# An encoder layer on one core: longer runs of wide matmuls in the feed-forward, merged products for its fourth tile, and another order of the last normalisation

## The chip, the cores and the metric

The kernel runs on one core of a Trainium2 chip. The metric is the device time of one execution in microseconds (us). A core has four compute engines with an instruction stream each: TensorE (PE in the profile, its weight loads PEld), VectorE (DVE), ScalarE (ACT) and GpSimd (POOL); SyncE (SP) issues most of the DMAs. SBUF is the on-chip memory, PSUM the eight banks of 512 f32 a partition into which TensorE accumulates.

## The reference, cut to what matters

One layer on 512 tokens of width 2048: a normalisation, an input projection, two token mixers side by side, an output projection, and then the gated feed-forward block with a width of 5632, which is where the change lies, and a last normalisation.

```python
    xn = rms_norm(x, ffn_norm_g[l])
    up = jnp.einsum("bsd,df->bsf", xn, w_up[l])
    up = depthwise_conv(up, ffn_dw_w[l], ffn_dw_b[l])
    gate, val = jnp.split(up, 2, axis=-1)
    x = x + jnp.einsum("bsf,fd->bsd", jax.nn.silu(gate) * val, w_down[l])
return rms_norm(x, final_norm_g)
```

## The kernel before, in words

All matrices are f32. Each operand is split in two parts, a high one in the rounded type that TensorE multiplies at full rate and a low one that holds the rest; a product is high x high + low x high + high x low. Weights come in units of 128 x 1024 values (512 KB): SyncE loads a unit `raw`, ScalarE copies its high part (`whi`, L117), VectorE subtracts to get the low part (`wlo`, L121). There are four buffers each for `whi` and `wlo`, and `weights()` makes units three ahead of the one in use. For some units VectorE first adds two raw ones (`ws`, L712 to L723).

**The up-projection.** The feed-forward runs over f = 0..43; each f is 128 gate and 128 value columns, and tokens are taken in two halves of 256. A scheme of the Strassen kind makes an f's four block products from seven products (0 to 6), each over eight k-steps. Its right-hand operands `xc` lie ready in SBUF, each k-step as 512 columns: the high part of 256 tokens beside their low part. There are two forms:

- `up` (merged): for each k-step one wide matmul of 512 columns (L773, the high weights times both parts at once) and one narrow matmul of 256 columns (L779, the low weights times the high part), which adds into the second half of the same bank. The halves are added later: ScalarE copies second halves out (`pl`, and `vv`; L805), and VectorE does eleven adds (L820 to L844). Within `up` the products go in runs: (0,1), (2,3), (4,5), (6). All but the last product of a run give their eight wide matmuls first; the last one gives one wide matmul, then come the narrow ones of the run, then the last product's other seven wide ones, so that a bank never closes with a narrow matmul of another.
- `up_apart`: three matmuls of 256 columns for each k-step (L131, L135, L136) into half a bank; three copies on ScalarE, six adds on VectorE (L879 to L885). It is used for f = 0 and f = 3.

A product's bank is one of three `mm` banks, the `po` bank or one of two `tr` banks (`product_bank`); from f = 4 on product 6 takes `po`, the others the `mm` banks.

**The down-projection.** Four f's are a chunk. While a chunk is worked, the four hidden tiles of the one before (each split in `hh` and `hl`, L911 and L912) are multiplied with `w_down`: behind product 3 and behind product 6 of each f one unit, which is two output tiles of 24 matmuls in all (`down`; L131 high x high, L135 high x low part `hl`, L136 low weights `wlo`), in the two `tr` banks. ScalarE copies each bank out (`pdc`, L926), and a GpSimd-queue DMA adds it to the sum in HBM (L927). The last chunk leaves out some of these places: f = 40 has none, f = 43 none behind product 3.

**The tail.** The last normalisation's factor is worked out by `spread` and 384 tokens are finished feature-major, in ten tiles on VectorE (L999) and six on GpSimd (L997); SyncE sends them to `out_T` in pairs (L1001, L1003). The other 128 tokens go to `out_N`. A planner orders each engine's instructions by priority and its own estimate of when operands are ready, so that rows move when code is written in another order; `pin` holds an instruction where the code has it.

## Time and profile before

| | |
|---|---|
| time, median of 3 runs (lowest, highest) | 2016.16 us (2015.9, 2017.13) |
| the profiled execution | 2016.15 us, its span 2014.4 us, 1.75 us outside the span |
| TensorE busy | 2004.4 us (100%) |
| VectorE busy | 1667.9 us (83%) |
| ScalarE busy | 1054.7 us (52%) |
| granted TensorE clock | 0.998 of full speed |
| wide matmuls of the up-projection | 2352, from 682.3 to 1937.0 us |

In the rows, a time is the start in us from the span's begin, followed by the duration in us; `x16` is a count; `pu<-xc,whi` reads "the tile pu is written from xc and whi"; a bracket at a row's end says how long the engine was idle before it and what released it. In the chain of waits each piece's length is the time to the next piece.

### The profile page before, as it was taken

To read this page: it belongs to the slowest core of one execution; us is meant where nothing else is said; L and a number is where in the kernel's file an instruction comes from. 1 tells how busy PE (TensorE), PEld (TensorE's weight loads), DVE (VectorE), ACT (ScalarE), POOL (GpSimd) and SP (SyncE) were. 2 spreads that over 40 slices of the span, in tenths; PEclk is the share of its full clock that TensorE was granted. 3 is DMA by queue.
4 is the path that set the end of the run, shared out by engine and by line. 5 is a ranking of instruction groups with operands and counts; after the bars stand their busy time and mean duration, and the time that the engine had idled before them with its cause. 6 is when DMAs were issued, how large, how long until landed. Compare 5 with 4: busy or idle time off the path is not lost.

```text
span 2014.4 us, 28027 instructions
## 1 busy us (share of the span) xinstructions
PE 2004.4 (100%) x10510; PEld 1715.7 (85%) x10510; DVE 1667.9 (83%) x2264; ACT 1054.7 (52%) x1689; POOL 169.4 (8%) x201
## 2 busy tenths in 40 slices
PE   9999999999999999999999999999999999999998
PEld 8888888888888998888888888888888888888887
DVE  7996888987576898887888888888888888889875
ACT  6323344476355665555555554555555555555563
POOL 0000000000002101111111111111111111110111
PEclk9999999999999999999999999999999999999999
DMA  7233333346348766556556556555565566564573
GB/s 258 84 106 93 113 95 107 105 139 211 100 136 213 189 163 152 139 129 152 133 135 148 131 131 154 132 139 141 127 145 145 127 145 147 131 141 128 145 206 129
DMA packets 98567, 284.25 MB, mean 141 GB/s; under 512 B 11008, under 2 KB 11520, under 8 KB 98432
## 3 DMA queue, kind: packets, MB, share of 16 engines
q1 hardware_dynamic: 71712, 231.07, 37.4%
q0 software_dynamic: 26720, 51.40, 17.1%
q8 instruction: 83, 1.36, 0.3%
q14 instruction: 52, 0.43, 0.1%
HBM read 227.90 MB, written 54.53 MB: 140 GB/s over the span
## 4 chain that ended last, share of the span: by engine, by line
PE 99%; DMA 0%; ACT 0%; DVE 0%; ACTq 0%; issue 0%; DVEq 0%
PE pu L773 27%; PE pu L779 14%; PE pd L136 8%; PE pd L131 8%; PE pd L135 8%; PE pj L131 6%; PE pj L135 6%; PE pj L136 6%; PE po L131 3%; PE po L135 3%; PE po L136 3%; PE pv L342 1%; PE pv L341 1%; PE pv L340 1%; PE po L535 1%; PE trp L518 1%
## 5 line engine op out<-in xcount | busy, mean ns | idle before, releaser
L117 ACT ACTIVATE whi<-raw 128x1024 fp32r<-128x1024 f32 x364 | 384.5, 1058 | 480.4 <-PE pj L135 131.7
L121 DVE TENSOR_TENSOR wlo<-raw,whi 128x1024 fp32r<-128x1024 f32 x364 | 444.5, 1222 | 208.5 <-ACT whi L117 198.0
L773 PE MATMUL pu<-xc,whi 128*128 128x512 f32 x2352 | 580.0, 391 | 0.0
L773 PEld LDWEIGHTS pu<-xc,whi 128*128 128x128 f32 x2352 | 433.5, 188 | 83.0
L779 PEld LDWEIGHTS pu<-xc,wlo 128*128 128x128 f32 x2352 | 306.8, 191 | 14.6
L779 PE MATMUL pu<-xc,wlo 128*128 128x256 f32 x2352 | 311.3, 283 | 0.0
L136 PE MATMUL pd<-hh,wlo 128*128 128x512 f32 x640 | 250.3, 391 | 0.0
L131 PE MATMUL pd<-hh,whi 128*128 128x512 f32 x640 | 249.7, 390 | 0.0
L135 PE MATMUL pd<-hl,whi 128*128 128x512 f32 x640 | 249.1, 390 | 0.0
L927 POOL DMA_DIRECT2D x2d<-pdc x160 | 138.9, 870 | 1099.0 <-ACT pdc L926 870.1
L131 PE MATMUL pj<-xh,whi 128*128 128x512 f32 x512 | 198.3, 392 | 0.1
L136 PE MATMUL pj<-xh,wlo 128*128 128x512 f32 x512 | 198.2, 390 | 0.0
L135 PE MATMUL pj<-xl,whi 128*128 128x512 f32 x512 | 198.2, 390 | 0.0
L805 ACT ACTIVATE pl<-pu 128x256 f32<-128x256 f32 x294 | 109.9, 382 | 150.1 <-PE pu L773 142.8
L117 ACT ACTIVATE whi<-ws 128x1024 fp32r<-128x1024 f32 x132 | 139.7, 1058 | 72.6 <-PE pu L773 54.2
L396 DVE SCALAR_TENSOR_TENSOR y<-ch,prm,y 128x501 f32<-128x501 f32 (+14 forms) x240 | 173.5, 740 | 4.4
L121 DVE TENSOR_TENSOR wlo<-ws,whi 128x1024 fp32r<-128x1024 f32 x132 | 161.2, 1221 | 14.8 <-ACT whi L117 14.8
L136 PEld LDWEIGHTS pd<-hh,wlo 128*128 128x128 f32 x640 | 120.1, 188 | 28.5 <-DVE wlo L121 3.3
L135 PEld LDWEIGHTS pd<-hl,whi 128*128 128x128 f32 x640 | 120.2, 188 | 25.0 <-DVE hl L912 0.4
L131 PEld LDWEIGHTS pd<-hh,whi 128*128 128x128 f32 x640 | 120.4, 188 | 22.6
L926 ACT ACTIVATE pdc<-pd 128x512 f32<-128x512 f32 x160 | 93.8, 588 | 79.1 <-PE pd L136 66.0
L131 PEld LDWEIGHTS pj<-xh,whi 128*128 128x128 f32 x512 | 96.0, 188 | 20.7 <-ACT g L276 0.3
(228 smaller groups left out, 2721.1 us busy)
## 6 DMA issues: line engine op xcount, KB each, us to landing
raw<-in_w_up SPq DMA_DIRECT2D x176, 512.0 KB, 3.9
raw<-in_w_down SPq DMA_DIRECT2D x88, 512.0 KB, 4.0
x2d<-pdc POOLq DMA_DIRECT2D x160, 256.0 KB, 4.8
raw<-in_w_in SPq DMA_DIRECT2D x60, 512.0 KB, 3.7
raw<-in_w_out SPq DMA_DIRECT2D x32, 512.0 KB, 3.6
raw<-in_w_v SPq DMA_DIRECT2D x16, 512.0 KB, 4.2
tab<-in_tab SPq DMA_DIRECT2D x32, 256.0 KB, 4.9
x<-in_xT SPq DMA_DIRECT2D x16, 256.0 KB, 6.1
```

Of the source, the lines that this page charges most:

```text
L117: i = nc.scalar.activation(hi[:, :n], raw[:, :n], AF.Copy)
L121: j = nc.vector.tensor_sub(lo[:, :n], raw[:, :n], hi[:, :n].bitcast(F32))
L131: m = nc.tensor.matmul(ps, hi[:, a], mh, start=start, stop=False)
L135: nc.tensor.matmul(ps, hi[:, a], ml, start=False, stop=False)
L136: return nc.tensor.matmul(ps, lo[:, a], mh, start=False, stop=stop)
L340: nc.tensor.matmul(ps, xh, wh[:, f], start=kk == 0, stop=False)
L396: nc.vector.scalar_tensor_tensor(y[:, a:b], h[:, a + j - PAD:b + j - PAD], prm[:, o + j:o + j + 1], y[:, a:b], op0=ALU.mult, op1=ALU.add)
L773: i = nc.tensor.matmul(ps, w[0][:, k * P:(k + 1) * P], comb[c][k], start=k == 0, stop=stop and k == ks[-1])
L779: i = nc.tensor.matmul(ps[:, H:], w[1][:, k * P:(k + 1) * P], comb[c][k][:, :H], start=False, stop=stop and k == U - 1)
L805: nc.scalar.activation(to, ps, AF.Copy)
L926: nc.scalar.activation(t, ps, AF.Copy)
L927: nc.gpsimd.dma_start(xd[d], t, accum_op=ALU.add)
```

## The change

There are four parts.

1. In `up`, from f = 4 on, the runs are (0,1,2,3) and (4,5,6) in place of (0,1), (2,3), (4,5), (6). Products 3 and 6 both take the `po` bank then, the others `mm`.
2. f = 3 uses `up` in place of `up_apart`, with the short runs.
3. `down` (in its usual form) opens both of its banks first, gives all sixteen matmuls with the high weights (L933 of the new file), and then the eight with the low weights (L943).
4. In `spread` for the tail, VectorE writes the factor to SBUF, and ScalarE copies it to PSUM; before, VectorE wrote it to PSUM and ScalarE copied it to SBUF. In `finish`, VectorE's first tile (d = 0) takes the factor from SBUF, its others take it from PSUM; GpSimd takes it from SBUF as before. ScalarE's scaling for d = 2 is held in its place.

```diff
@@ spread
+        nc.vector.scalar_tensor_tensor(r, q, 1.5, r, op0=ALU.add, op1=ALU.mult)
         if both:
-            nc.vector.scalar_tensor_tensor(ps, q, 1.5, r, op0=ALU.add, op1=ALU.mult)
-            nc.scalar.activation(r, ps, AF.Copy)
+            nc.scalar.activation(ps, r, AF.Copy)
             return ps, r
-        nc.vector.scalar_tensor_tensor(r, q, 1.5, r, op0=ALU.add, op1=ALU.mult)
         return r
@@ product_bank
-        at = n % 6 if f < CH else 3 * (c == 6)
+        at = n % 6 if f < CH else 3 * (c % 3 == 0 and c > 0)
@@ up
+        runs = ((0, 1), (2, 3), (4, 5), (6,)) if f < CH else ((0, 1, 2, 3), (4, 5, 6))
...
-            if c == 6:
+            run = next(r for r in runs if c in r)
+            if len(run) == 1:
                 ps = bank(c)
                 wides(c, w, ps, range(U - 1))
                 lows(c, w, ps)
                 i = wides(c, w, ps, range(U - 1, U), stop=True)
-            elif c % 2:
+            elif c == run[-1]:
                 ps = opened.pop(c)
                 lows(c, w, ps)
                 i = wides(c, w, ps, range(1, U), stop=True)
             else:
-                ps, opened[c + 1] = bank(c), bank(c + 1)
-                wides(c, w, ps, range(U))
-                wides(c + 1, made[weights.at], opened[c + 1], range(1))
+                if c == run[0]:
+                    for j in run:
+                        opened[j] = bank(j)
+                        wides(j, w if j == c else made[weights.at + j - c - 1], opened[j],
+                              range(1 if j == run[-1] else U))
+                ps = opened.pop(c)
                 i = lows(c, w, ps, stop=True)
@@ hidden
-        return gated_tile(f, *(up_apart if f == CH - 1 else up)(f, between))
+        return gated_tile(f, *up(f, between))
@@ down
-            for d in range(d0, d0 + U // CH):
-
-                ps = (psm.tile([P, S], F32, tag="mm", name="pd") if wide and d % 5 > 1 else
-                      psa.tile([P, S], F32, tag="tr", name="pd", bufs=2))
+            two = range(d0, d0 + U // CH)
+            banks = [] if wide else [bank(d) for d in two]
+            for ps, d in zip(banks, two):
                 for k in range(CH):
-                    mm3(ps, w, (d - d0) * CH + k, *hs[k], k == 0, k == CH - 1)
+                    a = slice(((d - d0) * CH + k) * P, ((d - d0) * CH + k + 1) * P)
+                    for i, x in enumerate(hs[k]):
+                        nc.tensor.matmul(ps, w[0][:, a], x, start=k + i == 0, stop=False)
+            for d in two:
+                if wide:
+                    ps = bank(d)
+                    for k in range(CH):
+                        mm3(ps, w, (d - d0) * CH + k, *hs[k], k == 0, k == CH - 1)
+                else:
+                    ps = banks[d - d0]
+                    for k in range(CH):
+                        a = slice(((d - d0) * CH + k) * P, ((d - d0) * CH + k + 1) * P)
+                        nc.tensor.matmul(ps, w[1][:, a], hs[k][0], start=False, stop=k == CH - 1)
@@ finish
-    def finish(pair, r, apart=False, split=False):
+    def finish(pair, rb, apart=False, split=False):
...
             if apart:
-                nc.scalar.activation(x, x, AF.Copy, scale=g)
-                nc.gpsimd.tensor_mul(o[:, i], x, r)
+                j = nc.scalar.activation(x, x, AF.Copy, scale=g)
+                if d == 2:
+                    pin(j)
+                nc.gpsimd.tensor_mul(o[:, i], x, rb[1])
             else:
-                nc.vector.scalar_tensor_tensor(o[:, i], x, g, r, op0=ALU.mult, op1=ALU.mult)
+                nc.vector.scalar_tensor_tensor(o[:, i], x, g, rb[d == 0], op0=ALU.mult, op1=ALU.mult)
```

How the order of instructions moves is shown at four places. The first is TensorE in an f from the middle of the feed-forward, before: the end of one down unit, products 0 to 3, and the beginning of the next down unit (`pd<-hh` is a hidden tile's high part, `pd<-hl` its low part).

```order
L136 MATMUL pd<-hh,wlo 128x512
L773 MATMUL pu<-xc,whi 128x512 x9
L779 MATMUL pu<-xc,wlo 128x256 x16
L773 MATMUL pu<-xc,whi 128x512 x16
L779 MATMUL pu<-xc,wlo 128x256 x16
L773 MATMUL pu<-xc,whi 128x512 x7
L131 MATMUL pd<-hh,whi 128x512
L135 MATMUL pd<-hl,whi 128x512
L136 MATMUL pd<-hh,wlo 128x512
```

The same place of an f after the change.

```order
L943 MATMUL pd<-hh,wlo 128x512 x8
L773 MATMUL pu<-xc,whi 128x512 x25
L779 MATMUL pu<-xc,wlo 128x256 x32
L773 MATMUL pu<-xc,whi 128x512 x7
L933 MATMUL pd<-hh,whi 128x512
L933 MATMUL pd<-hl,whi 128x512
```

Two runs of sixteen narrow matmuls became one of 32, and the low weights' matmuls of a down unit, which stood as every third one, stand at its end in one run of eight. Behind products 4 to 6 the same holds: before, it is 16 and 8 narrow ones, after, 24.

The second place is TensorE at the first down unit of the feed-forward, behind product 3 of f = 4, before the change, with buffer numbers: `hl_6633` is the low part of the fourth hidden tile (f = 3), `pd_6739` and `pd_6755` are the two banks.

```order
L131 MATMUL pd_6755<-hh_6628,whi_6665 128x512
L135 MATMUL pd_6755<-hl_6629,whi_6665 128x512
L136 MATMUL pd_6755<-hh_6628,wlo_6666 128x512
L135 MATMUL pd_6739<-hl_6633,whi_6665 128x512
L136 MATMUL pd_6739<-hh_6632,wlo_6666 128x512
L131 MATMUL pd_6755<-hh_6632,whi_6665 128x512
```

After the change, the same place; there `hl_6592` is the fourth tile's low part, `pd_6698` and `pd_6699` are the banks.

```order
L933 MATMUL pd_6699<-hh_6591,whi_6642 128x512
L773 MATMUL pu_6741<-xc_4982,whi_6657 128x512
L933 MATMUL pd_6698<-hl_6592,whi_6642 128x512
L933 MATMUL pd_6699<-hl_6592,whi_6642 128x512
L943 MATMUL pd_6698<-hh_6579,wlo_6643 128x512
L943 MATMUL pd_6698<-hh_6583,wlo_6643 128x512
```

The first matmul that wants the fourth tile's low part was the 20th of the unit's 24 before. Now it is the 15th, and one wide matmul of product 4 is drawn forward in front of it, so that it has fifteen matmuls of the unit's time ahead of it.

The third place is VectorE at the end of f = 3, before the change: the adds of `up_apart` and the weights around them.

```order
L879 TENSOR_TENSOR vl<-vv,pu 128x512
L723 TENSOR_TENSOR ws<-ws,raw 128x1024
L881 TENSOR_TENSOR uu<-uu,pu 128x256
L882 TENSOR_TENSOR vl<-vl,uu 128x512
L121 TENSOR_TENSOR wlo<-ws,whi 128x1024
L121 TENSOR_TENSOR wlo<-raw,whi 128x1024
L883 TENSOR_TENSOR vv<-vv,uu 128x256
L121 TENSOR_TENSOR wlo<-ws,whi 128x1024
```

After the change, the same place.

```order
L824 TENSOR_TENSOR vv<-vv,pl 128x512
L722 TENSOR_TENSOR ws<-ws,raw 128x1024
L831 TENSOR_TENSOR uu<-pu,pl 128x256
L834 TENSOR_TENSOR uu<-pu,pl 128x256
L832 TENSOR_TENSOR vl<-vv,uu 128x512
L121 TENSOR_TENSOR wlo<-ws,whi 128x1024
L121 TENSOR_TENSOR wlo<-raw,whi 128x1024
L837 TENSOR_TENSOR uu<-uu,pu 128x256
L121 TENSOR_TENSOR wlo<-ws,whi 128x1024
```

From the first row of it up to the fourth tile's low part (L912 before, L916 after) VectorE has five adds more than before, and two weight adds (L712 and L719 before) in other places.

The last place is VectorE's own first tiles of the tail, before, with the factor `st` in PSUM.

```order
L202 TENSOR_SCALAR st<-q,rstd_18246 128x384
L999 TENSOR_SCALAR fin<-x_17681,prm,st 128x384
L999 TENSOR_SCALAR fin<-x_17683,prm,st 128x384
L999 TENSOR_SCALAR fin<-x_17689,prm,st 128x384
L999 TENSOR_SCALAR fin<-x_17691,prm,st 128x384
```

And after.

```order
L201 TENSOR_SCALAR rstd_18205<-q,rstd_18205 128x384
L1020 TENSOR_SCALAR fin<-x_17640,prm,rstd_18205 128x384
L1020 TENSOR_SCALAR fin<-x_17642,prm,st 128x384
L1020 TENSOR_SCALAR fin<-x_17648,prm,st 128x384
L1020 TENSOR_SCALAR fin<-x_17650,prm,st 128x384
```

The first tile has the factor `rstd` in SBUF as its operand, the others `st` in PSUM, which ScalarE fills now. On GpSimd the first two tiles changed places (d = 3 ahead of d = 2); SyncE's order is the same.

More of the change, by code (lines that the diff above doesn't have):

```diff
@@ L915, in down, with bank @@
     def down(hs, ds, wide=False):
+        def bank(d):
+            return (psm.tile([P, S], F32, tag="mm", name="pd") if wide and d % 5 > 1 else
+                    psa.tile([P, S], F32, tag="tr", name="pd", bufs=2))
         for d0 in ds:
             w = weights()
-            for d in range(d0, d0 + U // CH):
-                ps = (psm.tile([P, S], F32, tag="mm", name="pd") if wide and d % 5 > 1 else
-                      psa.tile([P, S], F32, tag="tr", name="pd", bufs=2))
+            two = range(d0, d0 + U // CH)
+            banks = [] if wide else [bank(d) for d in two]
+            for ps, d in zip(banks, two):
                 for k in range(CH):
-                    mm3(ps, w, (d - d0) * CH + k, *hs[k], k == 0, k == CH - 1)
+                    a = slice(((d - d0) * CH + k) * P, ((d - d0) * CH + k + 1) * P)
[11 more added lines that the diff above has]
+                        nc.tensor.matmul(ps, w[1][:, a], hs[k][0], start=False, stop=k == CH - 1)
                 t = t2("pdc")
@@ L1032, in along @@
             pairs.remove(at)
-            finish(at, rb[at % 3 == 1], at % 3 == 1, at in (0, 2))
+            finish(at, rb, at % 3 == 1, at in (0, 2))
     for g, ps in enumerate(banks):
```

## The prediction

> **What bounds the kernel now.** The page's head, the busy times and the chain that ended last come first, then the line view of the wide matmuls.
>
> ```profile
> span 2014.4 us, 28027 instructions
> PE 2004.4 (100%) x10510; PEld 1715.7 (85%) x10510; DVE 1667.9 (83%) x2264; ACT 1054.7 (52%) x1689; POOL 169.4 (8%) x201
> PE 99%; DMA 0%; ACT 0%; DVE 0%; ACTq 0%; issue 0%; DVEq 0%
> L773 PE MATMUL pu<-xc,whi x2352: 389/389/404, 682.3 to 1937.0; 128*128 128x512 f32 x196
> ```
>
> TensorE is the chain: 99% of the span. An edit counts by the matmuls it removes, by what a matmul costs beyond its columns, and by the waits of TensorE that it makes or takes. So the chain is read next, piece by piece: a piece's length is the time to the next piece. Here are f = 2 (merged, short runs), f = 3 (apart), and the start of f = 4; and, as a ruler, nine wide matmuls inside a down unit's end.
>
> ```profile
> 701.78 2.29 PE pu L773 x10
> 704.07 1.91 PE pu L779 x16
> 705.98 3.65 PE pu L773 x16
> ...
> 717.12 3.20 PE pu L773 x14
> 720.32 0.95 PE pu L779 x8
> 721.27 0.23 PE pu L773
> 721.62 0.12 PE pu L135
> ...
> 741.06 0.12 PE pu L135
> 741.66 2.07 PE pu L773 x9
> ...
> 819.11 2.04 PE pu L773 x9
> ```
>
> A wide matmul takes 2.04 / 9 = 0.227 us, a narrow one 0.12. f = 3 takes 168 x 0.12 = 20.16 us (721.50 to 741.66). A merged f has 56 of each: 56 x (0.2267 + 0.12) = 19.41. f = 2 lasts from 701.78 to 721.50, 19.72 us; its pieces are 57 wide and 56 narrow, 12.92 + 6.72 = 19.64. The rest, 0.08 us over four runs of narrow matmuls, is 0.02 us a run, whether the run has 8 or 16. Between first and last wide matmul there were 4176 wide matmuls (the down-projection's have the same 512 columns) and 2520 narrow ones in 187 runs: 1249.0 us without any extra, against 1937.0 - 682.3 = 1254.7. So 5.7 us are extras: 187 x 0.02 = 3.7 and about 1.9 in waits. The view of waits and the chain around one of them say where those lie.
>
> ```profile
> PEld pd L136 <- DVE wlo L121: 3.3, 9, 0.4
> 841.71 0.23 PE pd L131
> 841.94 0.43 PE pd L136
> 842.37 0.23 PE pd L131
> ```
>
> Nine times a down unit's third or fourth matmul wants low weights that VectorE has not yet made. Weight loads run ahead of matmuls, so the 3.3 us of that row are not all lost: in the chain the piece is 0.43 instead of 0.23, 0.20 us lost, and nine times that is 1.8. With the rest above (5.7 - 3.7) I take 1.9.
>
> **The change, part by part.** (a) *f = 3 merged.* 20.16 becomes 19.41: -0.75 us, and its four runs are in (b). ScalarE gets six more copies of 256 columns and VectorE five more adds; ScalarE was busy for 10.22 of f = 3's 20 us (row below), so its part costs nothing; VectorE's part is (d).
>
> (b) *Longer runs.* From f = 4 on there are 2 runs instead of 4 in each of 40 f's, or 80 fewer; some others go because the order no longer draws wide matmuls into narrow runs; f = 3 adds its own. Counted in the order, 187 become 94 over the whole stretch, 93 x 0.02 = -1.9 us. The bounds are 0 (the 0.02 might belong to each bank rather than to a switch) and -1.9; f = 2's rest is the same in every run, so I take -1.9.
>
> (c) *Low weights last in a down unit.* They are wanted sixteen matmuls, 3.6 us, later than the high ones instead of 0.5 us later. The lateness was 0.2 us each: all nine waits go, -1.9 us. Late next would be the units of a run: the first product's wide matmuls ask for four high parts within 25 matmuls (5.7 us), where they asked for two within 9, and TensorE could catch up with ScalarE's copies. ScalarE is little loaded and VectorE has 5 us idle in a usual f (24.88 busy of 30):
>
> ```profile
> 721.00:741.00 20.00, 20.00 (x168) 19.96 (x167) 18.86 (x26) 10.22 (x14) 1.74 (x2) 1.00 0.71 178
> 741.00:772.00 31.00, 31.00 (x166) 26.56 (x165) 30.64 (x41) 17.51 (x29) 2.61 (x3) 1.00 0.55 155
> 772.00:802.00 30.00, 30.00 (x160) 25.93 (x159) 24.88 (x32) 16.40 (x25) 3.47 (x4) 1.00 0.62 138
> 1845.00:1860.00 15.00, 15.00 (x91) 13.34 (x90) 14.93 (x21) 8.32 (x12) 0.00 (x0) 1.00 0.43 133
> ```
>
> (The columns: stretch, length, then the busy time of PE, PEld, DVE, ACT and POOL, TensorE's clock, DMA share, GB/s.) Walked through with the durations of the rows below, the parts of a usual f come 6 us and more ahead of their matmuls; no cost.
>
> (d) *The new wait, at f = 4.* From 721 to 772 us VectorE has hardly any idle time (18.86 of 20, 30.64 of 31), and five adds are put in ahead of the fourth hidden tile's low part, which f = 4's first down unit now wants as its fifteenth matmul. VectorE's rows there, before, and TensorE's:
>
> ```profile
> 721.34 0.28 PE L131 MATMUL pu<-xc,whi 128*128 128x256 f32 x1
> 733.09 0.68 DVE L879 TENSOR_TENSOR vl<-vv,pu 128x512 f32<-128x512 f32 x1
> 738.21 1.22 DVE L121 TENSOR_TENSOR wlo<-raw,whi 128x1024 fp32r<-128x1024 f32 x1
> 739.35 0.42 DVE L883 TENSOR_TENSOR vv<-vv,uu 128x256 f32<-128x256 f32 x1
> 739.68 1.22 DVE L121 TENSOR_TENSOR wlo<-ws,whi 128x1024 fp32r<-128x1024 f32 x1
> 742.62 0.68 DVE L903 TENSOR_TENSOR vl<-vl,rstd 128x512 f32<-128x512 f32 x1
> 743.22 0.69 DVE L902 TENSOR_TENSOR g<-g,rstd 128x512 f32<-128x512 f32 x1
> 746.09 0.75 DVE L893 SCALAR_TENSOR_TENSOR uy<-g,prm,uy 128x511 f32<-128x511 f32 x1
> 746.75 0.75 DVE L893 SCALAR_TENSOR_TENSOR uy<-vl,fwn,uy 128x511 f32<-128x511 f32 x1
> 753.42 0.69 DVE L912 TENSOR_TENSOR hl<-uy,hh 128x512 fp32r<-128x512 f32 x1
> 754.21 0.44 PE L135 MATMUL pd<-hl,whi 128*128 128x512 f32 x1
> ```
>
> From start to start, VectorE takes 1.14 us for 1024 columns (738.21 to 739.35), 0.60 for 512 (742.62 to 743.22), 0.33 for 256 (739.35 to 739.68) and 0.66 for a convolution step (746.09 to 746.75). In the order after, from the add that takes the place of 733.09's to the end of the fourth low part, stand ten of 1024, ten of 512, seven of 256, four convolution steps and the low part itself (0.69): 11.4 + 6.0 + 2.3 + 2.6 + 0.7 = 23.0, so it is done at 756.1. TensorE: f = 3 from 721.34, 19.49 with its four runs, f = 4 from 740.83; then 32 wide and 32 narrow matmuls (11.09 + 0.02), so the down unit begins at 751.94, and the matmul in question, fifteen matmuls on, is due at 755.34. A matmul starts 0.1 us after such a writer's end (753.42 + 0.69 to 754.21), and its piece was 0.1 longer than a wide one's: 756.2 + 0.1 - 755.34 = 1.0 us. Bounds: 0 (VectorE had gaps of its own before, up to 1.1 us, which the walk may have too little or too much of) and 2 (one more 1024-column step in front, 1.14). I take +1.0; it is the middle, and the walk gives it. Behind the waiting matmul stand the eight low-weights ones and f = 4's products 4 to 6; all slide by the same 1.0, paid once.
>
> (e) *The tail.* In order: VectorE's factor, GpSimd's and VectorE's tiles, SyncE's first DMAs, and the stretch in which the DMA engines stand still once more.
>
> ```profile
> 1998.31 0.57 DVE L202 SCALAR_TENSOR_TENSOR st<-q,rstd 128x384 f32<-128x384 f32 x1
> 1999.49 3.24 DVE L999 SCALAR_TENSOR_TENSOR fin<-x,prm,st 128x384 f32<-128x384 f32 x6 [0.62 <-ACT rstd L203]
> 1999.55 2.98 POOL L997 TENSOR_TENSOR fin<-x,rstd 128x384 f32<-128x384 f32 x3 [36.60 <-ACT rstd L203]
> 2000.14 0.86 SPq L1001 DMA_DIRECT2D out_T<-fin  x2
> 2001.58 0.33 SPq L1003 DMA_DIRECT2D out_T<-fin  x1
> 2002.00:2003.00 1.00, 1.00 (x8) 0.83 (x8) 1.00 (x3) 0.52 (x2) 1.00 (x2) 1.00 0.68 260
> ```
>
> Both engines waited for ScalarE's copy; the factor itself was there at 1998.88. VectorE's first tile can now start 0.58 us earlier (1999.49 to 1998.91), and so the first DMA. The end is set by the transfers, which run without a break from 2001 on but for 0.32 us in the last row. That break is the third DMA's: it waits in SyncE's order for GpSimd's second tile (1999.55 + 2 x 1.0 = 1.55, issue at 1.58). So the tail gets shorter only as GpSimd gets earlier. If GpSimd starts at 1998.9 too, it is -0.55 us; if it starts at 1999.5 as before, the first DMAs' gain becomes a longer break and it is 0. No row has VectorE and GpSimd both starting on two SBUF operands (VectorE's tiles read the factor from PSUM), so neither end is excluded; I take 0, the nearest row's start.
>
> The Trainium skill (SBUF — State Buffer, "Who interferes with whom") speaks against a gain: a VectorE instruction with two SBUF inputs and a GpSimd instruction that reads SBUF share a port, the first to issue holds it for its whole length, and the other stands still. By that rule the new first tile (two SBUF inputs, some 0.6 us) would hold GpSimd back to about 1999.5 and (e) would be 0; without it -0.55. No run here shows it yet.
>
> **The sum.** -0.75 - 1.9 - 1.9 + 1.0 + 0 = -3.5 us on the profiled execution's 2016.15 (2014.4 in the span, 1.75 around it), which is the median of the runs, 2016.16, within 0.01: 2012.7 us. A measurement of this kernel can tell about 0.2%, 4.0 us, from no change: the bounds are 2012.1 and 2020.2.
>
> **The rivals.** *GpSimd starts at once* (e at -0.55): 2012.1. For it: its operand is there at 1998.9. Against it: VectorE's tile starts in the same moment.
>
> *No wait at f = 4* (d at 0): 2011.7; with the former, 2011.1. For it: before, the order put late work at places where TensorE waited only 0.1 us. Against it: the walk, in which VectorE has nothing left to give.
>
> *The runs save nothing* (b at 0): 2014.5. Against it: f = 2's 0.08 us. [...]
>
> *More waits where VectorE is full* (1 to 3 us more, at f = 4's other products and at f = 40, where it is busy for 14.93 of 15 us): 2014 to 2016.
>
> *Slower: the shared `po` bank.* Products 3 and 6 both use it. Product 6's first wide matmul, which now stands at the head of the second run, waits until VectorE's add of product 3 (L834 after) has read it. In a usual f: the low matmuls of the down unit end 11.1 + 5.4 = 16.5 us after the f's start; only then is a `wlo` buffer free, and VectorE gives a low part, an add of 512 and L834 (1.14 + 0.60 + 0.33): 18.6. Product 6's matmul stands sixteen wide ones behind the down unit: 16.5 + 3.6 = 20.2. A slack of 1.5 us. If VectorE falls more than 1.5 us behind that walk in each of the 38 f's with a down unit there, each 0.25 us beyond it costs 9.5 us in all: 2012.7 + 9.5 = 2022. It decides from 0.2 us in each f. For it: VectorE is the second busiest engine, and the nine waits of before show it late at just this place. Against it: its 5 us of idle time in an f.
>
> **How the numbers follow.** The forecast (2012.7, by itself 2012.0 to 2013.6) has 0.33, of which 0.06 lies below 2012.1; GpSimd at once 0.24, half of it below; no wait at f = 4 0.20, all below; the runs save nothing 0.05; more waits 0.08; the bank 0.10. Faster by over 0.2%: 0.06 + 0.12 + 0.20 = 0.38; slower 0.10; within, 0.52. The range 2011.0 to 2015.5 leaves out the bank, the upper part of the waits (0.03) and what lies below both gains together (0.04).
>
> **What would show it.** (a) f = 3 taking 19.5 us in the chain. (b) 94 narrow runs with pieces of 32 and 24 whose lengths are 0.12 a matmul plus 0.02. (c) No row of TensorE waiting for `wlo`. (d) One piece near 755 us of about 1 us more, with `hl` as releaser. (e) GpSimd's first tile at its factor's end plus 0.6 or at once, and the break in the transfers. The prediction is wrong if TensorE waits in each f, at `po` or for a unit's high part.

## The result

The changed kernel takes 2013.44 us (median of 20 runs, 2012.49 to 2015.14) against 2016.78 us of the kernel before (20 runs, 2015.9 to 2017.85). The ratio is 0.9984, with a 95% interval of 0.9978 to 0.9990: 0.16% or 3.3 us faster, which is inside the 0.2% that were called "no change", though clear of noise. The forecast was 2012.7, by -3.5 us, with a range of 2011.0 to 2015.5.

The profiled execution took 2013.1 us with a span of 2011.2. The page's head and the line view of the wide matmuls, of the kernel after:

```profile
span 2011.2 us, 27994 instructions
PE 2000.8 (99%) x10454; PEld 1714.0 (85%) x10454; DVE 1660.8 (83%) x2269; ACT 1067.9 (53%) x1695; POOL 171.4 (9%) x201
PE 96%; DVE 2%; issue 1%; ACT 1%; ACTq 0%; POOL 0%; DVEq 0%; POOLq 0%
L773 PE MATMUL pu<-xc,whi x2408: 389/389/467, 682.5 to 1933.6; 128*128 128x512 f32 x186
```

TensorE is still the bound. The span divides at three points: the first wide matmul of the up-projection, the last one, and the moment at which VectorE has the tail's factor (in the kernel after, 1995.49; its row stands below).

| stage | before | after |
|---|---|---|
| up to the first wide matmul | 682.3 | 682.5 |
| first to last wide matmul | 1254.7 | 1251.1 |
| last wide matmul to the tail's factor | 61.9 | 61.9 |
| factor to the span's end | 15.5 | 15.7 |

All of the gain lies between the first and the last wide matmul. Part four, in the tail, brought nothing and even 0.2 us less. One f from the chain of waits, after:

```profile
802.84 5.67 PE pu L773 x25
808.51 3.83 PE pu L779 x32
812.34 1.61 PE pu L773 x7
813.96 3.63 PE pd L933 x16
817.58 1.81 PE pd L943 x8
819.39 3.85 PE pu L773 x17
823.25 2.87 PE pu L779 x24
826.12 1.61 PE pu L773 x7
827.74 3.63 PE pd L933 x16
831.36 1.81 PE pd L943 x8
```

Ten pieces of the up-projection and the down-projection follow each other without a gap, and the 25 and 17 wide matmuls have the same 0.227 us as before. The narrow pieces hold no extra (3.83 and 2.87 us, 0.12 a matmul); the 0.02 us lie behind them, in the seven wide matmuls that follow (1.61 us where 7 x 0.2267 = 1.59). The prediction looked for them in the narrow pieces themselves. The row of TensorE's waits that named the down-projection's low weights, nine times, is gone; in its place there is one of the hidden tile's low part, and the timeline of TensorE around it shows where:

```profile
PEld pd L933 <- DVE hl L916: 1.2, 2, 0.7
754.60 0.50 PE L933 MATMUL pd<-hl,whi 128*128 128x512 f32 x1
755.63 0.40 PE L773 MATMUL pu<-xc,whi 128*128 128x512 f32 x1
756.34 0.73 PE L933 MATMUL pd<-hl,whi 128*128 128x512 f32 x2 [0.31 <-DVE hl L916]
```

The fourth tile's matmuls start at 756.34, 0.71 us behind the wide matmul ahead of them where 0.23 is usual; with the third tile's smaller wait of 0.2 us ahead of 754.60, and 0.11 us more than usual for the first matmul behind each of the two waits, TensorE loses 0.9 us there.

### The profile page after: what moved, and what is told of

The parts are those of the page before. It is cut to its first block, busy times and chain, and to the rows that moved or that the text cites. A ratio compares the mean times of both kernels' runs of the same rounds, so it can differ in the third digit from the quotient of the medians.

```text
span 2011.2 us, 27994 instructions
## 1 busy us (share of the span) xinstructions
PE 2000.8 (99%) x10454; PEld 1714.0 (85%) x10454; DVE 1660.8 (83%) x2269; ACT 1067.9 (53%) x1695; POOL 171.4 (9%) x201
## 4 chain that ended last, share of the span: by engine, by line
PE 96%; DVE 2%; issue 1%; ACT 1%; ACTq 0%; POOL 0%; DVEq 0%; POOLq 0%
PE pu L773 25%; PE pd L933 14%; PE pu L779 13%; PE pd L943 7%; PE pj L131 6%; PE pj L135 6%; PE pj L136 6%; PE po L131 3%; PE po L136 3%; PE po L135 3%; PE pv L340 1%; PE pv L341 1%; PE pv L339 1%; PE pd L131 1%; PE pd L136 1%; PE pd L135 1%
## 5 line engine op out<-in xcount | busy, mean ns | idle before, releaser
L773 PEld LDWEIGHTS pu<-xc,whi 128*128 128x128 f32 x2408 | 446.2, 188 | 89.0 <-issue 0.2
L779 PEld LDWEIGHTS pu<-xc,wlo 128*128 128x128 f32 x2408 | 301.3, 191 | 7.2
L779 PE MATMUL pu<-xc,wlo 128*128 128x256 f32 x2408 | 303.6, 283 | 0.0
L933 PE MATMUL pd<-hl,whi 128*128 128x512 f32 x608 | 236.6, 389 | 0.4 <-DVE hl L916 0.3
L933 PE MATMUL pd<-hh,whi 128*128 128x512 f32 x608 | 236.4, 389 | 0.0
L943 PE MATMUL pd<-hh,wlo 128*128 128x512 f32 x608 | 150.2, 389 | 0.0
L933 PEld LDWEIGHTS pd<-hl,whi 128*128 128x128 f32 x608 | 114.1, 188 | 24.8 <-DVE hl L916 1.2
L943 PEld LDWEIGHTS pd<-hh,wlo 128*128 128x128 f32 x608 | 114.1, 188 | 23.7
L933 PEld LDWEIGHTS pd<-hh,whi 128*128 128x128 f32 x608 | 114.1, 188 | 23.6
L136 PEld LDWEIGHTS pj<-xh,wlo 128*128 128x128 f32 x512 | 96.1, 188 | 20.4 <-DVE wlo L236 0.2
```

The lines of the kernel that those rows point to most:

```text
L136: return nc.tensor.matmul(ps, lo[:, a], mh, start=False, stop=stop)
L773: i = nc.tensor.matmul(ps, w[0][:, k * P:(k + 1) * P], comb[c][k], start=k == 0, stop=stop and k == ks[-1])
L779: i = nc.tensor.matmul(ps[:, H:], w[1][:, k * P:(k + 1) * P], comb[c][k][:, :H], start=False, stop=stop and k == U - 1)
L933: nc.tensor.matmul(ps, w[0][:, a], x, start=k + i == 0, stop=False)
L943: nc.tensor.matmul(ps, w[1][:, a], hs[k][0], start=False, stop=k == CH - 1)
```

## The experiments

The times' intervals are some 0.1% (2 us) to either side, so the small differences are read from the traces, where two stages repeat well: from the first to the last wide matmul, and from the tail's factor to the span's end. Each kernel has one profile, and starts are shown to 0.1 us, so a difference of two entries is good to about 0.1. The time up to the first wide matmul, which no part touches, lies anywhere from 682.3 to 683.8 us in these profiles; that alone moves the total time by over 1 us.

| kernel | median us | ratio to before, interval | first to last wide | factor to end |
|---|---|---|---|---|
| before | 2016.7 | 1 | 1254.7 | 15.5 |
| after | 2013.44 | 0.9984 [0.9978, 0.9990] | 1251.1 | 15.7 |
| e1_short_runs | 2029.06 | 1.0061 [1.0048, 1.0074] | 1266.4 | 15.5 |
| e2_down_old | 2012.01 | 0.9978 [0.9969, 0.9987] | 1250.0 | 15.2 |
| e3_f3_apart | 2013.05 | 0.9980 [0.9971, 0.9989] | 1250.9 | 15.0 |
| e5_single_runs | 2016.92 | 1.0000 [0.9992, 1.0009] | 1254.4 | 15.4 |
| e4_tail_old | 2014.45 | 0.9986 [0.9977, 0.9994] | 1251.7 | 15.8 |
| e6_all_psum | 2014.67 | 0.9989 [0.9980, 0.9998] | 1251.7 | 15.5 |
| e7_send_later | 2013.85 | 0.9984 [0.9975, 0.9992] | 1251.1 | 15.9 |
| e9_short_runs_po | 2014.58 | 0.9985 [0.9977, 0.9994] | 1253.7 | 15.0 |
| b1_long_runs | 2012.98 | 0.9980 [0.9971, 0.9989] | 1251.0 | 15.2 |
| b3_low_last | 2027.71 | 1.0053 [1.0039, 1.0067] | 1267.1 | 15.2 |
| e10_warm | 2012.50 | 0.9981 [0.9972, 0.9990] | 1251.1 | 15.0 |
| e11_all | 2010.83 | 0.9970 [0.9959, 0.9982] | 1250.2 | 14.4 |

### What a run of narrow matmuls costs: seven runs for an f

```diff
-        runs = ((0, 1), (2, 3), (4, 5), (6,)) if f < CH else ((0, 1, 2, 3), (4, 5, 6))
+        runs = ((0, 1), (2, 3), (4, 5), (6,)) if f < CH else tuple((c,) for c in range(7))
```

> The changed kernel with seven runs of one product each from f = 4 on: 292 runs of narrow matmuls, of 8 each, where the changed kernel has 94, the suspected cost three times over with the same matmuls. Theory (0.02 us a run): 198 x 0.0196 = 3.9 us more, first to last wide matmul 1255.0, time 2017.3. Rival (the extra belongs to something else than the switch of width, such as the length of the runs or the banks): less than 1 us more.

Measured: 1254.4 us from first to last wide matmul, 3.3 more than the changed kernel, of which the wait at f = 4 takes back 0.4 (it was 0.5 us here). From the counts: 1254.4 - 0.5 - 1248.35 (4232 wide and 2408 narrow matmuls) leaves 5.55 us for 292 runs, 0.019 each. In the chain of this kernel each run of eight costs its own excess over eight matmuls and the following wide ones:

```profile
803.42 1.59 PE pu L773 x7
805.01 0.95 PE pu L779 x8
805.96 1.84 PE pu L773 x8
807.80 0.95 PE pu L779 x8
808.75 1.84 PE pu L773 x8
```

From 805.01 to 807.80 are eight narrow and eight wide matmuls: 2.79 us where 8 x 0.12 + 8 x 0.2267 = 2.77. The 0.02 us belong to a switch of width and not to a run's length or its bank. Nor do they belong to the change from high to low weights: a down unit of the changed kernel makes that change at one width, and its 24 matmuls above (813.96 to 819.39) take 5.43 us where 24 x 0.2267 = 5.44. The rival, under 1 us, falls. The Trainium skill (TensorE: Matmul & The Clock Gate, "Back-to-back issue gap") gives an isolated matmul's gap by its own columns alone, and says of a stream that the weight load and the matmul set the spacing together. Neither statement has a term for a switch of width, and here 198 further runs with the same matmuls cost 3.7 us.

### Which part took the waits away: parts one and three undone, and each alone

Part three undone, with the old `down` in the changed kernel:

```diff
     def down(hs, ds, wide=False):
...
+            for d in range(d0, d0 + U // CH):
+                ps = (psm.tile([P, S], F32, tag="mm", name="pd") if wide and d % 5 > 1 else
+                      psa.tile([P, S], F32, tag="tr", name="pd", bufs=2))
                 for k in range(CH):
...
-                    for i, x in enumerate(hs[k]):
-                        nc.tensor.matmul(ps, w[0][:, a], x, start=k + i == 0, stop=False)
...
+                    mm3(ps, w, (d - d0) * CH + k, *hs[k], k == 0, k == CH - 1)
```

> The changed kernel with its third part undone: in a down unit the low weights' matmuls stand as every third one again. Theory: TensorE waits for VectorE's low weights in some of the f's again, 0.1 to 0.2 us lost each time, and the wait of 0.9 us for the fourth hidden tile at f = 4 becomes smaller, since the first matmul that wants it stands later in the unit. First to last wide matmul 1251.1 becomes 1251.5 to 1253 and the view of waits shows wlo as what the down-projection's weight loads wait for, 5 to 40 times. Rival (the waits came from the short runs, which left VectorE less time ahead of the down unit, so that the order in the unit does not matter): no such row, and 1250.2 to 1251.1.

The rival had it right: no row of TensorE waiting for `wlo` in the down-projection, and 1250.0, 1.1 us less than the changed kernel. The wait at f = 4 is gone as well, and its 0.9 us are nearly all of the 1.1. So with long runs part three saves nothing and, beside a merged f = 3, costs the wait at f = 4. That part one is enough by itself was tried on the kernel before:

```diff
-        at = n % 6 if f < CH else 3 * (c == 6)
+        at = n % 6 if f < CH else 3 * (c % 3 == 0 and c > 0)
...
+        runs = ((0, 1), (2, 3), (4, 5), (6,)) if f < CH else ((0, 1, 2, 3), (4, 5, 6))
...
```

> The kernel before with the first part of the change alone: the runs (0,1,2,3) and (4,5,6) and their banks; f = 3 apart, the low weights as every third matmul of a down unit, the tail as before. In the order it has 91 runs of narrow matmuls instead of 188. Theory A (the nine waits for low weights came from the short runs, which put the down unit's low weights close behind two units that VectorE had yet to make): no wait for low weights, first to last wide matmul 1249.1 + 91 x 0.0196 = 1250.9, against 1254.7 before; time 2013.0. Theory B (as predicted, the waits go only when the low weights stand last in the down unit): the waits of 0.2 us stay, nine or more, 1252.7; time 2014.8.

Theory A: 1251.0, 3.7 us less than before, and no wait for low weights. The chain where one of the nine waits stood (841.94 before) has a long run and a down unit without one:

```profile
834.13 5.67 PE pu L774 x25
839.80 3.83 PE pu L780 x32
843.63 1.61 PE pu L774 x7
845.24 0.23 PE pd L131
```

The opposite, part three without part one, was run on both kernels. First by undoing part one in the changed kernel:

```diff
-        at = n % 6 if f < CH else 3 * (c % 3 == 0 and c > 0)
+        at = n % 6 if f < CH else 3 * (c == 6)
...
-        runs = ((0, 1), (2, 3), (4, 5), (6,)) if f < CH else ((0, 1, 2, 3), (4, 5, 6))
+        runs = ((0, 1), (2, 3), (4, 5), (6,))
```

> The changed kernel with its first part undone: runs (0,1), (2,3), (4,5), (6) for every f, and only product 6 in the po bank. In the order this has 191 runs of narrow matmuls between the first and the last wide one where the changed kernel has 94, with the same number of matmuls. Theory (each run costs 0.02 us whatever its length): 97 x 0.0196 = 1.9 us more between first and last wide matmul, 1251.1 becomes 1253.0, and the time 2015.3. Rival (a change of width costs nothing): 1251.1 as now. A second rival (the shared po bank made TensorE wait, so that the short runs are no worse): at or below 1251.1.

Every one of these expectations missed: 1266.4, 15.3 us more than the changed kernel, where 1.9 were expected. The waits of TensorE's weight loads in this kernel, and then VectorE's timeline and TensorE's weight loads at one of the 38 places:

```profile
PEld pu L773 <- issue: 14.4, 38, 0.5
PEld pu L773 <- ACT pl L809: 5.4, 18, 0.4
```

```profile
787.69 1.23 DVE L121 TENSOR_TENSOR wlo<-ws,whi 128x1024 fp32r<-128x1024 f32 x1
792.09 1.23 DVE L121 TENSOR_TENSOR wlo<-raw,whi 128x1024 fp32r<-128x1024 f32 x1 [3.18 <-PE pd L943]
793.24 0.42 DVE L831 TENSOR_TENSOR uu<-pu,pl 128x256 f32<-128x256 f32 x1
793.77 0.19 PEld L773 LDWEIGHTS pu<-xc,whi 128*128 128x128 f32 x1 [0.38 <-issue]
```

VectorE stands still for 3.18 us, until the down unit's last low-weight matmul (L943) has been done and its `wlo` buffer is free. Behind the low part that it then makes stands the add L831, which reads product 2's bank; product 5 has the same bank with the short runs' numbering, and its first wide matmul (the weight load at 793.77, 0.11 us behind the add's end at 793.66) waits for it. The profile puts the wait down to "issue", but the times name the add: in all 38 places the weight load starts 0.11 to 0.12 us behind the end of L831. The proof is the same kernel with another bank:

```diff
-        runs = ((0, 1), (2, 3), (4, 5), (6,)) if f < CH else ((0, 1, 2, 3), (4, 5, 6))
+        runs = ((0, 1), (2, 3), (4, 5), (6,)) if f < CH else ((0, 1), (2, 3), (4, 5), (6,))
```

> The changed kernel with short runs (0,1), (2,3), (4,5), (6), as in the run with the short runs, but with the changed kernel's banks: products 3 and 6 in po, so that product 5 no longer takes the bank of product 2. With short runs and product 5 in product 2's bank, first to last wide matmul was 1266.4, and TensorE stood before product 5's first wide matmul in each f. The reading of that: VectorE waits 3.2 us for a buffer for the next low weights, which the down unit releases only at its end, and its add that reads product 2's bank stands behind that wait. Theory: with the other banks that wait goes, and what stays are 172 runs x 0.02 and the wait at f = 4: 1248.4 + 3.4 + 0.9 = 1252.7, the time 2015.0. Rival (TensorE waits for the units themselves, which come too late with short runs and the new down unit): 1260 or more.

Measured 1253.7, 12.7 us less than with the other banks and 1.0 above the expected 1252.7: the waits in each f are gone, and one wait for `po` came, a single time, at f = 40 (where the prediction had found VectorE full):

```profile
PEld pu L773 <- DVE uu L834: 1.7, 1, 1.7
```

And part three alone on the kernel before, with the numbering of before (the new `down`, all else as before):

```diff
+            banks = [] if wide else [bank(d) for d in two]
+            for ps, d in zip(banks, two):
                 for k in range(CH):
-                    mm3(ps, w, (d - d0) * CH + k, *hs[k], k == 0, k == CH - 1)
...
+                    for i, x in enumerate(hs[k]):
+                        nc.tensor.matmul(ps, w[0][:, a], x, start=k + i == 0, stop=False)
...
```

> The kernel before with the third part of the change alone: both banks of a down unit opened, the low weights' eight matmuls last. Theory A (the low-weight buffer is released only at the unit's end, VectorE stands still for it, and its read of product 2's bank, which product 5 wants next, is late in each f): first to last wide matmul 12 to 14 us more than the 1254.7 before, TensorE standing 0.2 to 0.4 us before product 5's first wide matmul in nearly each f; time 2029. Theory B (as predicted for this part: the nine waits go, nothing comes in their place): 1252.8 and 2014.3.

1267.1 and 2027.71 us: Theory A, 12.4 us more than the kernel before from the first to the last wide matmul. Again 38 waits before a wide matmul:

```profile
PEld pu L774 <- issue: 16.8, 38, 2.6
PEld pu L774 <- ACT pl L810: 5.4, 18, 0.4
```

So the third part is bearable only with the banks of the first one, which keep VectorE's late reads away from TensorE. In all three kernels with short runs and part three (e1_short_runs, e9_short_runs_po, b3_low_last) no wait for the down-projection's low weights is left. So each of the two parts removes the nine waits by itself, and the change removes them twice over.

### The wait at f = 4: part two undone

```diff
-        return gated_tile(f, *up(f, between))
+        return gated_tile(f, *(up_apart if f == CH - 1 else up)(f, between))
```

> The changed kernel with its second part undone: f = 3 has its three matmuls of 256 columns for each k-step and five adds fewer on VectorE. Theory: f = 3 takes 0.75 us more (20.16 instead of 19.41, less 0.08 for its four runs), and TensorE's wait of 0.9 us at f = 4's first down unit goes, because VectorE has 2.0 to 2.5 us less to do ahead of the fourth hidden tile's low part: first to last wide matmul 1251.1 becomes 1250.9, and the time is the same within 0.3 us. Rival (the wait at f = 4 comes from the new order of the down unit alone, whatever f = 3 does): the wait stays at 0.5 to 1 us and the sum is 1251.5 to 1251.9.

1250.9, as the theory has it: f = 3 is 0.67 us longer, the wait is gone. The chain at f = 4 has sixteen matmuls of the down unit in one piece, 3.70 us, 0.07 above sixteen times 0.227:

```profile
752.19 1.61 PE pu L773 x7
753.80 3.70 PE pd L933 x16
757.50 1.82 PE pd L943 x8
```

Since the wait also goes with the old `down` (e2_down_old), it needs both: the five adds that make VectorE late and the new order that wants their result early. In the changed kernel's order it was 0.9 us in three profiles (after, e7_send_later, e10_warm) and 1.5 in two others (e4_tail_old and e6_all_psum, hence their 1251.7); these five differ only at the program's start and in the tail, and why the wait differs stays open. So parts two and three together lose what part two gains. Part three by itself costs nothing where f = 3 is apart: 1250.9 here against 1251.0 in b1_long_runs.

### The tail

Part four undone (`spread` and `finish` as before):

```diff
+        if both:
+            nc.vector.scalar_tensor_tensor(ps, q, 1.5, r, op0=ALU.add, op1=ALU.mult)
+            nc.scalar.activation(r, ps, AF.Copy)
+            return ps, r
         nc.vector.scalar_tensor_tensor(r, q, 1.5, r, op0=ALU.add, op1=ALU.mult)
-        if both:
-            nc.scalar.activation(ps, r, AF.Copy)
-            return ps, r
         return r
...
-                nc.vector.scalar_tensor_tensor(o[:, i], x, g, rb[d == 0], op0=ALU.mult, op1=ALU.mult)
+                nc.vector.scalar_tensor_tensor(o[:, i], x, g, r, op0=ALU.mult, op1=ALU.mult)
...
```

> The changed kernel with its fourth part undone: the factor is written to PSUM by VectorE and copied to SBUF by ScalarE, and all of VectorE's tiles read it in PSUM. In the changed kernel's profile the third DMA of the tail is issued 2.53 us after the factor's end, and 2.70 before the change, and the span ends 15.67 us after the factor, 15.51 before. Theory (the gain of the first DMAs is lost again in a longer break before the third): third DMA at 2.70, end 15.2 to 15.7 us after the factor, no difference in the time beyond 0.4 us. Rival (part four is worth the 0.5 us by which VectorE starts earlier): the time 0.5 us longer.

The third DMA goes out at 2.70 and the end is 15.75 us after the factor, 0.08 later than with the new tail. The time differs by 1.0 us (2014.45), but in the two profiles 0.7 lie ahead of the first wide matmul, 0.6 in the wait at f = 4 and only 0.1 in the tail. To see where the earlier start went, here are the changed kernel's rows of VectorE, GpSimd and SyncE:

```profile
1994.93 0.56 DVE L201 SCALAR_TENSOR_TENSOR rstd<-q,rstd 128x384 f32<-128x384 f32 x1
1995.53 0.62 DVE L1020 SCALAR_TENSOR_TENSOR fin<-x,prm,rstd 128x384 f32<-128x384 f32 x1
1995.63 1.39 POOL L1018 TENSOR_TENSOR fin<-x,rstd 128x384 f32<-128x384 f32 x1 [37.07 <-DVE rstd L201]
1996.17 0.87 SPq L1022 DMA_DIRECT2D out_T<-fin  x2
1998.02 1.00 SPq L1024 DMA_DIRECT2D out_T<-fin  x1
```

VectorE and GpSimd start together, 0.04 and 0.14 us after the factor. GpSimd's first tile lasts 1.39 us where it takes 1.01 otherwise; and SyncE's third issue lasts 1.00 where 0.33 was usual. Two causes, then, and each has its own run. The first, by giving VectorE's first tile the factor in PSUM:

```diff
-                nc.vector.scalar_tensor_tensor(o[:, i], x, g, rb[d == 0], op0=ALU.mult, op1=ALU.mult)
+                nc.vector.scalar_tensor_tensor(o[:, i], x, g, rb[0], op0=ALU.mult, op1=ALU.mult)
```

> The changed kernel, but VectorE's first tile of the tail reads the factor from PSUM like its others; GpSimd still reads VectorE's SBUF factor without ScalarE in between. In the changed kernel GpSimd's first tile took 1.39 us and its others 1.01, while VectorE's first tile with two SBUF operands ran. Theory (that tile held GpSimd back): GpSimd's first tile takes 1.0 us, its second ends 2.1 us after the factor, the third DMA is issued at 2.2 instead of 2.53; VectorE's first tile starts 0.6 after the factor instead of 0.04. The break in the transfers becomes shorter by 0.8 us and lies in front of them instead; the time changes by -0.4 to 0. Rival (the first tile is long for another reason, such as GpSimd's long idle time before it): 1.39 us again and the third DMA at 2.5.

GpSimd's first two tiles take 2.02 us together, the first one 1.01, and GpSimd ran beside VectorE's tiles from 1997.92 on without being stretched:

```profile
1997.50 2.02 POOL L1018 TENSOR_TENSOR fin<-x,rstd 128x384 f32<-128x384 f32 x2 [35.78 <-DVE rstd L201]
1997.92 1.66 DVE L1020 SCALAR_TENSOR_TENSOR fin<-x,prm,st 128x384 f32<-128x384 f32 x3 [0.56 <-ACT st L203]
```

So it is the SBUF factor of VectorE's tile that held GpSimd back, by 0.38 us of the 0.51 in which the two overlap. The first tile takes 1.39 to 1.40 in all nine profiles with such a VectorE tile beside it and 1.01 to 1.03 in the other five. That is the rule of the Trainium skill (SBUF — State Buffer, "Who interferes with whom") weighed in the prediction, and the trace agrees: 1.39 us beside a tile with two SBUF operands, 1.01 beside tiles with one. The profile shows the hold as a longer instruction, not as a later start. VectorE's second SBUF operand was also the very tile that GpSimd reads; no run gives the two engines different ones, so that the sharing of one tile is not excluded. The third DMA, however, did not go out at 2.2 but at 2.93, since now the second issue was long. The other attempt, sending VectorE's second pair first, met the same thing:

```diff
+    later = []
...
-        if not split:
+        if pair == 1:
+            later.append(o)
+        elif not split:
             nc.sync.dma_start(out[pair], o)
+        if pair == 2:
+            nc.sync.dma_start(out[1], later.pop())
```

> The changed kernel, but SyncE sends GpSimd's first pair behind VectorE's second pair instead of ahead of it; nothing else is moved. Theory (the transfers of the tail set its end, and the break in them comes from the third DMA waiting for GpSimd): the third and fourth DMA, now VectorE's, go 1.8 and 2.4 us after the factor, the break of 1.3 us in the transfers shrinks to under 0.3, the span ends 14.6 us after the factor instead of 15.67, and the time is 1.0 us shorter. Rival (the end is set by GpSimd's last tiles or by the token-major outputs): 15.2 to 15.7 us as now.

The third DMA went out at 1.73 as foreseen and the fourth at 3.82, because the issue of the third took 1.99 us. The end was 15.85, not 14.6. In all seven profiles in which one of the first four issues was stretched so (after, e1, e2, e4, e5, e6, e7) a packet of 16 KB on the instruction queue (q8) lies in the tail, and the issue ends 0.32 to 0.39 us after the packet does: in after, the packet runs from 1.64 to 3.16 us after the factor, and the issue ends at 3.53; in e7 3.35 and 3.72. The DMA view of 1996 to 2000 us of the changed kernel (each digit is 0.1 us) shows the packet's row and the break:

```profile
DMA  0000000000799797999882000011010100089998
q8 instruction: 1, 0.02, 2.4%
```

Such packets come, on average, once in about 255 records of TensorE and its weight loads (21196 records and 83 packets in after). With twenty fewer there should be no packet in the tail:

```diff
-    for _ in range(16):
-        pin(nc.tensor.matmul(ps[:, 0, :H], warm[:, :P], warm, start=True, stop=True))
+    for _ in range(6):
+        pin(nc.tensor.matmul(ps[:, 0], warm[:, :P], warm, start=True, stop=True))
```

> The changed kernel with the sixteen idle matmuls of 256 columns at the program's start replaced by six of 512 columns, 10 matmuls and 10 weight loads fewer; they compute nothing that is used. In the profiles a packet of 16 KB on the instruction queue comes about every 255 instructions of TensorE; with the change the last one falls 1.64 us after the tail's factor and lasts 1.5 us, and the DMA that SyncE issues meanwhile takes until 0.37 us after that packet's end (0.52 to 1.99 us instead of 0.34). The run with short runs and the changed banks had 18 TensorE instructions fewer and no such packet, and its span ended 15.0 us after the factor instead of 15.67. Theory (the packet stretches the issue): with 20 instructions fewer it is gone, the third DMA's issue takes 0.34 us, the span ends 15.0 us after the factor; the time is 0.7 us shorter, give or take what the shorter start does. Rival (the stretched issue comes from the transfers in flight): 15.2 to 15.8 as now.

No packet of that queue after the factor, SyncE's issues 0.33 to 0.44 us long up to the seventh, and 15.0 us from the factor to the end:

```profile
1997.96 0.33 SPq L1024 DMA_DIRECT2D out_T<-fin  x1
1998.39 0.90 SPq L1022 DMA_DIRECT2D out_T<-fin  x2
```

The median is 0.9 us below the changed kernel's, though the two intervals overlap; the 0.7 us in the tail are read from the traces. The three kernels without a packet there and with the new tail (e3, e9, e10) all have 15.0; those with the old tail and no packet have 15.5, 15.2 and 15.2 (before, b1, b3). Part four alone is thus worth 0.2 to 0.5 us; the old tails differ by 0.3 among themselves, for a reason that stays open. Merging f = 3 takes 56 matmuls and their weight loads out of TensorE's stream: the last packet lies 8.3 to 8.8 us ahead of the factor in the four kernels with f = 3 apart, and 1.6 behind it in the changed kernel, where the tail is 0.7 us longer than in e3_f3_apart.

Last, what the runs had shown, put together: the old `down`, the later sending of GpSimd's pair, and the six idle matmuls (the edits shown above).

> The changed kernel with what the runs showed put together: the down units in the order of before (every third matmul with the low weights), GpSimd's first pair of the tail sent behind VectorE's second pair, and the six idle matmuls at the start. Theory: first to last wide matmul 1250.0 as in the run with the old down unit (1.1 us less than the changed kernel), and the tail's transfers run without a break once no packet of instructions falls among them: the span ends 14.3 us after the factor instead of 15.67. Time 2013.4 - 1.1 - 1.4 = 2010.9. Rival (the tail's end is set by its last outputs, so that the order of the first ones is worth nothing): 15.0 after the factor, 2011.6.

2010.83 us, 0.30% below the kernel before (interval 0.18 to 0.41%) and 2.6 us below the changed one, 0.9 and 1.3 us of which lie in the two stages of the table. First to last wide matmul 1250.2, and in the tail the first four issues go out one after another:

```profile
1995.78 1.91 SPq L1009 DMA_DIRECT2D out_T<-fin  x4
1997.00:1998.00 1.00, 1.00 (x6) 0.82 (x5) 1.00 (x3) 0.00 (x0) 1.00 (x2) 1.00 1.03 364
1998.00:1999.00 1.00, 1.00 (x8) 0.83 (x8) 1.00 (x3) 0.30 (x1) 1.00 (x2) 1.00 1.05 381
1999.00:2000.00 1.00, 1.00 (x6) 0.82 (x6) 1.00 (x3) 0.39 (x2) 1.00 (x2) 1.00 1.02 396
```

The transfers have no break (DMA share 1.02 to 1.05), and the end is 14.4 us after the factor, 14.3 having been forecast. The rival's 15.0 falls. The same order of sending with a packet in the tail (e7_send_later) had 15.85, so that there the packet costs 1.4 us.

## Why the prediction was right, and where it was not

The size was right: -3.3 us measured, -3.5 forecast, and the time in the range. By its steps:

- (a) *f = 3 merged*, -0.75: undoing it costs 0.67 us in f = 3 (20.16 less 19.49). Right.
- (b) *Longer runs*, -1.9: right; 0.019 us a run, measured with 292 runs of eight and 94 of 8 to 32. The extra lies in the wide matmuls behind a run, not in the run's own piece.
- (c) *Low weights last*, -1.9: the waits went, but this part was not needed for it. Here the step failed. It argued from how much later the low weights are wanted and did not ask whether the longer runs of the same change would already give VectorE that time. They did: part one alone saves 3.7 us, (b) and the nine waits together. Part three would have removed the waits too, with short runs, but in this change it had nothing left to save and cost 1.1 us, nearly all of it the wait of (d). The step's "no cost", from a walk in which VectorE waits for a `wlo` buffer, held in a usual f only because of part one's banks; with the old ones part three costs 12.4 us.
- (d) *The wait at f = 4*, +1.0: 0.9 in the profile of after. The walk had VectorE done at 756.1 and TensorE's matmul 0.1 later, at 756.2; they came at 756.28 and 756.34. The term was booked to f = 3's five adds and the new order together, and it needs both: with either of them undone (e3_f3_apart, e2_down_old) the wait is gone. In two other profiles of the same code it was 1.5.
- (e) *The tail*, 0: +0.2 measured, made of a gain of 0.2 to 0.5 and a packet of instructions in the wrong place, which no step had. That it came out near 0 was luck. That GpSimd would be held by VectorE's first tile was true and worth 0.38 us of GpSimd's time, where the prediction expected its start 0.6 later; it started at once, took longer, and the third DMA went out 0.17 us earlier (2.53 instead of 2.70).
- The rival with the shared `po` bank: its slack was forecast at 1.5 us; in the changed kernel product 6's first wide matmul starts 1.48 us after L834's end in 36 of the 40 f's from f = 4 on. At f = 4, 40 and 41 only 0.14 to 0.18 us are left, and at f = 40 TensorE waits there for 0.2 us, a single time; in e9_short_runs_po it was 1.7.

The sum hid the mistake in (c), since the waits went whichever part took them: a sum that comes out does not show that each term has the right owner. Only doing each part alone did.

## What to carry to other kernels

A matmul order that releases a weight buffer later is not free where the engine that fills the buffer has other work queued behind that wait: look up which PSUM bank its next instruction reads and who wants that bank. When several parts of a change can each remove the same wait, run each alone before booking the gain. A switch between two matmul widths had a small fixed cost here (0.02 us), and so long runs of one width paid.

## What the runs showed of the hardware that was not expected

- A 16 KB packet on the instruction queue, on average once in about 255 records of TensorE and its weight loads, stretched a DMA issue of SyncE from 0.33 us to 0.5 to 2.0: the issue under way ended 0.32 to 0.39 us after the packet in each of seven profiles, and no issue among the first four was stretched in the seven without a packet there. A packet alone does not do it. Over the whole of the 14 traces, 355 SyncE issues meet a packet within their usual 0.33 us; 54 of them took over 0.5 us, and each of the 54 was begun within 1.5 us of the end of the issue before it. Of the 263 that were begun later than that, none was stretched, and nearly all of the weight units' issues (`raw`), spaced widely, are among these. In a tail set by transfers a packet was worth 0.2 us (e2_down_old against e3_f3_apart) to 1.4 (e7_send_later against e11_all), and 18 and 20 instructions fewer in TensorE's stream (e9_short_runs_po, e10_warm) were enough to keep it out. Why one packet takes 0.9 us and another 1.7, and why the issue waits for it, stays open.
- GpSimd's tile with an SBUF operand took 1.39 us beside a VectorE tile with two SBUF operands and 1.01 beside VectorE tiles with a PSUM operand.
